# An encoder block's opening written out as one list of small operations, with form stores and K's sum column placed by hand

## Chip, cores and metric

The kernel runs on one core of a Trainium2 chip. The metric is device time in microseconds (us) of one execution; the time before is the median of 3 runs.

## What is computed

One encoder block on x of shape (1, 1024, 1024) in float32. Only the first stage bears on this change:

```python
u = rms_norm(x, norm1_g)                     # row scale, then per-column gain
proj = u @ w_in                              # 1024 x 5120
q, k, v, cb, cc, ch, ga, gb = split(proj)    # q, k, v: 512 columns each
q = rms_norm(q.reshape(B, S, 8, 64), q_norm_g)
k = rms_norm(k.reshape(B, S, 8, 64), k_norm_g)
y_a = neighbourhood_attention(q, k, v, rpb) @ w_attn_branch
...
x = x + (sigmoid(ga) * y_a + sigmoid(gb) * y_b) @ w_o
x = x + square(relu(rms_norm(x, norm2_g) @ w_mlp_in)) @ w_mlp_out
```

## The kernel before

Every float32 operand of a matmul is split into two float16 parts, high and low, and a product is three passes: high by high, high by low, low by high (`PASSES`, L473). A weight is first scaled by a power of two that is found from the weight itself: for V from the largest absolute value of the matrix (`largest`, L327), for Q and K from its sum of squares (L256 to 269). Either number is brought from 128 partitions to one by a product with an all-ones matrix (`all_sum`, L197), read back by DVE and turned into a scale.

The opening computes V, then Q, then K for the 1024 rows, in 8 blocks of 128. For each block (`norm`, L447): ACT squares and sums the row, DVE and ACT make the row scale, ACT writes the high half of the scaled row (`hi`) and DVE the low half (`lo`), into `u16`. Blocks 0 to 2 are transposed on TensorE (PE) and copied out of PSUM, the high half by ACT and the low half by DVE (`ln_trans`, L457); blocks 3 to 7 are transposed by a DMA on SP's queue (`ln_turn`, L469). The result, `UT`, is the stationary operand of everything that follows. V's weights come in two column halves of two pieces each; Q's in four pieces. V's first three blocks are computed in two half groups of 24 matmuls of 256 columns, since the second half of the weights is split later; blocks 3 to 7 in full groups of 24 matmuls of 512 columns (`v_unit`, L535); Q's and K's blocks in full groups (L643 to 652). ACT and DVE read a group out of PSUM into a high and a low part (`post`, L539).

Beside this, four "forms" are made of the scaled rows for a later stage (`sforms`, L500): ACT scales two blocks of x in place, POOL makes four sums of 512 columns, ACT and DVE split them, SP stores 1 MB to DRAM. There is one buffer for the sums and two for their split.

The order on each queue is the order in which the Python program emits instructions. It is made by generators: `bg` holds the preparation of weights (`Chunk.prep`, L250), advanced by `tick`; `fg` holds row work, forms and the read-out of Q and K (`qk_vec`, L607), advanced by `step`; `unit` (L204) emits a group of matmuls and then so many steps and ticks. `apart` (L179) holds a generator until a count of units has passed. L547 to L594 spell out the opening in such steps. Weights arrive in a ring of five buffers (`rawp`, L77; `load_upto`, L231), filled by SP in order. Waits between engines are inserted by the framework where an instruction needs another's result or a buffer.

Of the kernel before, what the change touches and what calls it, by code (L numbers as in the profile page):

```python
# [10 lines left out]
F32 = mybir.dt.float32  # L11
# [17 lines left out]
def plan():  # L29
# [19 lines left out]
    return p  # L49

# [20 lines left out]
def encoder_block(ctx: ExitStack, tc: tile.TileContext, x, weights, cols, gqk, rel, masks, out):  # L71
# [167 lines left out]
    class Chunk:  # L239
# [10 lines left out]
        def prep(self):  # L250
# [5 lines left out]
            if self.kind in "QKCG":  # L256
# [10 lines left out]
                yield from apart(units[0], 2 if self.kind in "QC" else 3)  # L267
# [179 lines left out]
    def norm(xin, sq, u, y):  # L447

        ss = tmp()
        A.activation(sq, xin, AF.Square, accum_out=sc[:, ss])  # L450
        yield
        yield from rstd(ss, D, y, 9)
        A.activation(u[:, 0], xin, AF.Copy, scale=sc[:, y])
        yield
        V.scalar_tensor_tensor(u[:, 1], xin, sc[:, y], u[:, 0], op0=OP.mult, op1=OP.subtract)

    def ln_trans(u16, b, dst):  # L457
        for s in range(2):
            pt = bank16("o")
            for k in range(8):  # L460
                T.transpose(pt[:, k * 128:(k + 1) * 128], u16[:, s, k * 128:(k + 1) * 128], ident)
            o = dst[:, s, :, b * 128:(b + 1) * 128]
            i = pt.rearrange("p (k t) -> p k t", k=8)
            if s == 0:
                A.activation(o, i, AF.Copy)
            else:
                V.tensor_copy(o, i)

    def ln_turn(u16, b, dst):  # L469
        SP.dma_start_transpose(dst[:, :, :, b * 128:(b + 1) * 128].rearrange("p s k t -> p (s k) t"),  # L470
                               u16.rearrange("p s k -> p (s k)"))

# [21 lines left out]
    ln = [norm(xt[:, b], sq, u16[:, b % 4], at(ys, b)) for b in range(8)]  # L494
    GS = dram.tile([128, 4, 4, 2, 512], F16, name="gs")

    turned, formed = [0], [0]
    SFORM = (6, 8, 10, 12)

    def sforms():  # L500

        for n, start in enumerate(SFORM):
            yield from apart(start, 0)
            assert turned[0] >= n + 5
            z = []
            for b in (n, n + 4):
                A.activation(xt[:, b], xt[:, b], AF.Copy, scale=sc[:, at(ys, b)])
                z += [xt[:, b, :512], xt[:, b, 512:]]
            f = wqk.tile([128, 4, 512], F32, name="sform", bufs=1)
            v = wqk.tile([128, 4, 2, 512], F16, name="s16", bufs=2)  # L510
            for o, a, b, op in ((2, z[0], z[2], OP.subtract), (0, z[2], z[3], OP.subtract),
                                (1, f[:, 0], z[0], OP.subtract), (3, z[1], f[:, 1], OP.add)):
                G.tensor_tensor(f[:, o], a, b, op=op)
            yield from apart(start, 2)
            A.activation(v[:, :, 0], f, AF.Copy)
            yield
            V.tensor_tensor(v[:, :, 1], f, v[:, :, 0], op=OP.subtract)
            fg.append(sform_store(n, v))

    def sform_store(n, v):  # L520
        yield from apart(units[0], 1)
        SP.dma_start(GS[:, n], v)
        formed[0] = n + 1

    def ln_step(b, n=1):
        for _ in range(n):
            advance(ln[b])
# [6 lines left out]

    def v_unit(b, j, steps, ticks):  # L535
        ps = bank("ds"[b % 2])
        n, c = (512, 0) if j is None else (256, 256 * j)

        def post():  # L539
            hi, lo = (VT[:, b, s, c:c + n] for s in range(2))  # L540
            A.activation(hi, ps[:, :n], AF.Copy, scale=2.0 ** -20)
            V.scalar_tensor_tensor(lo, ps[:, :n], 2.0 ** -20, hi, op0=OP.mult, op1=OP.subtract)
        w = vhome[0] if j is None else vhome[0][:, j]
        unit(group(ps[:, :n], [(UT[:, sa, k, b * 128:(b + 1) * 128], w[..., sw, k * 256:(k + 1) * 256])
                               for k in range(8) for sa, sw in PASSES]), post, steps, ticks)
# [12 lines left out]
    ln_step(1, 5)
    ln_step(1)
    ln_step(2, 2)  # L560
    push(cV[1])
    tick(1)
    v_unit(0, 0, 0, 0)
    ln_step(2, 4)
    ln_trans(u16[:, 1], 1, UT)
    ln_step(2, 1)
    tick(3)
    ln_step(2)
    tick(4)
    ln_step(3, 2)  # L570
    ln_trans(u16[:, 2], 2, UT)
    ln_step(3, 4)
    fg.append(qk_gain())
    fg.append(sforms())
    V.tensor_reduce(sc[:, gm2], sc[:, g1], axis=AX, op=OP.max, apply_absolute_value=True)
    mul(gm2, gm2, gm2)
    for p in range(11):
        if p == 3:
            flush()
            push(cQ)  # L580
        if 0 < p < 6:
# [1292 lines left out]
```

## Time and profile before

| | us |
|---|---|
| time, median of 3 runs | 1239.75 |
| the runs | 1237.73 to 1241.18 |
| the profiled execution's own time | 1236.77 |
| its span, first to last instruction | 1235.0 |
| PE busy | 1196.9 |
| DVE busy | 936.9 |
| ACT busy | 765.9 |
| POOL busy | 430.3 |

A view lists groups or single instructions. PE is TensorE's matmuls, PEld its weight loads, DVE VectorE, ACT ScalarE, POOL GpSimd, SP the queue that issues DMAs. A row of the view in order of time is start, duration, engine, line, operation, output<-input, shape and count; the bracket tells how long the engine stood idle before it and what ended that. L66 and L207 are lines of helpers, so operations are told apart by the names of their tiles: `xt` is x, `u` the split rows, `uT` their transpose, `w_v` and `w_ws` split weights of V and of Q or K, `vT` the split V, `sform` and `s` a form and its split. A group's row ends with total busy time, mean ns of one, and idle time before. The busy time of matmuls is modelled at their ends, so the distance between starts is the better measure.

### The profile page before, as it was taken

What the parts mean: (1) busy time and instruction counts of PE and PEld (TensorE: products, weight loads), DVE (VectorE), ACT (ScalarE), POOL (GpSimd) and SP (SyncE); (2) the same over time, 40 slices, a digit from 0 to 9 for tenths busy, and PEclk for the clock granted to TensorE, in tenths of its full rate; (3) what the DMA queues carried; (4) which work ended last, traced back from release to release, by engine and by line L of the source; (5) the groups of instructions that cost most, each with busy time, mean ns of one, the idle gap of its engine ahead of it and who ended that gap; (6) DMA issues with size and microseconds to landing.
All of it is one profiled execution on the core that took longest, in us unless ns stands there. A gap on an engine that the chain in (4) does not pass through costs nothing.

```text
span 1235.0 us, 16691 instructions
## 1 busy us (share of the span) xinstructions
PE 1196.9 (97%) x6102; PEld 576.9 (47%) x6102; DVE 936.9 (76%) x1747; ACT 765.9 (62%) x1185; POOL 430.3 (35%) x289
## 2 busy tenths in 40 slices
PE   5989999999899999999999999999999999999998
PEld 3534445555444444444458444444444444444444
DVE  6668778888558786877878664555547999999997
ACT  6777667768644454535768777777775763646430
POOL 2440003232212111101003466655648373463562
PEclk8999999999899999999999999999999999999999
DMA  6558455565761211216096653454474844435202
GB/s 258 107 200 178 103 118 112 116 153 105 131 154 34 69 52 51 69 35 255 18 174 152 205 170 137 162 187 142 140 290 162 313 155 159 168 116 222 103 35 103
DMA packets 170867, 173.34 MB, mean 140 GB/s; under 512 B 131488, under 2 KB 132000, under 8 KB 166688
## 3 DMA queue, kind: packets, MB, share of 16 engines
q1 hardware_dynamic: 170784, 172.27, 47.2%
q8 instruction: 48, 0.79, 0.3%
q14 instruction: 35, 0.29, 0.1%
HBM read 102.51 MB, written 37.75 MB: 114 GB/s over the span
## 4 chain that ended last, share of the span: by engine, by line
PE 40%; DVE 6%; ACT 2%; issue 2%; DMA 1%; DVEq 0%; ACTq 0%
PE ps_d L207 16%; PE ps_s L207 14%; PE ps_o L207 10%; DVE as L66 1%; DVE ops L66 1%; DVE w L66 1%; DVE form L66 1%; ACT as L66 1%; DVE v L66 1%; DMA u2T<-v 1%; DMA u2x<-v 1%; ACT ops L66 1%; DVE x L66 0%; DVE sc L66 0%; ACT u2x L66 0%
## 5 line engine op out<-in xcount | busy, mean ns | idle before, releaser
L207 PEld LDWEIGHTS <-ops 128*128 128x128 f16 x1356 | 132.4, 98 | 159.9 <-issue 2.7
L207 PEld LDWEIGHTS <-w 128*128 128x128 f16 x1368 | 132.8, 98 | 143.5 <-issue 3.8
L924 PE MATMUL ps_d<-uT,w_ws 128*128 128x512 f16 x576 | 136.7, 382 | 0.0
L207 PE MATMUL ps_s<-ops 128*128 128x512 f16 (+1 forms) x528 | 118.3, 374 | 0.0
L207 PE MATMUL ps_d<-ops 128*128 128x512 f16 x504 | 115.6, 379 | 0.0
L66 ACT ACTIVATE ops<-hf,sc 128x2048 f16<-128x2048 f32 x26 | 52.0, 1999 | 94.0 <-PE ps_d L207 52.7
L207 PE MATMUL ps_d<-u2T,w 128*128 128x512 f16 (+1 forms) x504 | 110.3, 371 | 0.0
L1074 POOL TENSOR_TENSOR tsum<-raw 128x512 f32<-128x512 f32 x28 | 46.6, 1677 | 148.1 <-ACT raw L66 148.1
L207 PEld LDWEIGHTS <-uT 128*128 128x128 f16 x648 | 64.9, 101 | 70.5 <-issue 5.6
L1278 POOL TENSOR_TENSOR as<-as 128x512 f32<-128x512 f32 x56 | 76.7, 1370 | 41.4 <-ACT as L66 38.1
L207 PEld LDWEIGHTS <-w_s 128*128 128x128 f16 x588 | 56.9, 98 | 68.6 <-DVE w_s L66 0.6
L924 PEld LDWEIGHTS <-w_ws 128*128 128x128 f16 x576 | 56.1, 98 | 59.7 <-issue 2.0
L207 PE MATMUL ps_s<-u2x,w 128*128 128x512 f16 (+1 forms) x348 | 78.6, 375 | 0.0
L207 PE MATMUL ps_o<-ops 128*128 128x512 f16 x324 | 74.3, 379 | 2.4 <-DVE as L66 2.4
L66 DVE SCALAR_TENSOR_TENSOR ops<-hf,sc,ops 128x2048 f16<-128x2048 f32 x26 | 71.7, 2759 | 5.7 <-ACT ops L66 5.7
L66 ACT ACTIVATE raw<-raw,sc 128x256 f32<-128x256 f32 x172 | 71.1, 494 | 6.7 <-DMA raw<-in_weights 6.7
L66 DVE TENSOR_TENSOR as<-ps_s,as 128x512 f32<-128x512 f32 (+1 forms) x38 | 23.4, 616 | 58.5 <-ACT as L66 57.9
L66 DVE TENSOR_SCALAR sc<-sc 128x1 int32<-128x1 int32 (+3 forms) x380 | 57.6, 167 | 12.9 <-ACT sq L66 4.3
L1074 POOL TENSOR_TENSOR gsum<-raw 128x512 f32<-128x512 f32 x14 | 18.5, 1340 | 136.8 <-issue 52.3
L66 ACT ACTIVATE w<-raw,sc 128x512 f16<-128x512 f32 (+1 forms) x29 | 25.4, 920 | 50.8 <-DVE sc L66 50.8
L66 ACT ACTIVATE sz<-sz,sc 128x384 f32<-128x384 f32 (+1 forms) x64 | 37.2, 581 | 26.8 <-DVE sc L66 26.6
L66 DVE SCALAR_TENSOR_TENSOR w_ws<-raw,sc,w_ws 128x512 f16<-128x512 f32 (+2 forms) x72 | 48.5, 712 | 6.7 <-ACT w_ws L66 6.7
(261 smaller groups left out, 2548.6 us busy)
## 6 DMA issues: line engine op xcount, KB each, us to landing
raw<-in_weights SPq DMA_DIRECT2D x89, 512.0 KB, 5.5
hs<-as SPq DMA_DIRECT2D x16, 1792.0 KB, 8.7
hf<-hs SPq DMA_DIRECT2D x26, 1024.0 KB, 6.7
w2x<-in_weights SPq DMA_DIRECT2D x16, 512.0 KB, 8.3
raw<-in_weights SPq DMA_DIRECT2D x16, 384.0 KB, 3.7
xt<-in_x SPq DMA_DIRECT2D x8, 512.0 KB, 9.8
gs<-s SPq DMA_DIRECT2D x4, 1024.0 KB, 6.4
x<-in_x SPq DMA_DIRECT2D x8, 512.0 KB, 10.0
```

Of the source, the lines that this page charges most:

```text
L66: return f(out, *a, **kw)
L207: T.matmul(ps, l, r, start=a, stop=b)
L924: T.matmul(ps, l, r, start=a, stop=b)
L1074: G.tensor_tensor(t[:, o], a, b, op=OP.add)
L1278: sub.tensor_tensor(z[o], z[a], z[b], op=op)
```

## The change

The generators of the opening (`norm`, `ln_trans`, `ln_turn`, `sforms`, `v_unit`, L547 to L594) go, and a string `BEGIN` names the small operations in the order in which they are emitted, V, forms and Q's first four groups together:

```text
sq.0 ts.0 sqrt.0 tr.0 y.0 tr.1 col.0 hi.0.P lo.0 Th.0 one.0 sq.1 ts.1 sq.2 scal.0 sqrt.1 y.1 ch.0.A
hi.1.P whi.0.1 whi.0.0 Tl.0 ts.2 tr.2 cl.0.V wlo.0.1.P V.0.0.hh.0 lo.1 Th.1 whi.1.0 sqrt.2 y.2 hi.2.P
whi.1.1 V.0.0.hh.1 ch.1.A sq.3 V.0.0.lh.0 V.0.0.lh.1 tr.3 Tl.1 col.1 V.1.0.hh.0 lo.2 wlo.0.0.P
V.1.0.hh.1 Th.2 cl.1.A sq.5 V.1.0.lh.0 wlo.1.0.P ch.2.V one.1 ts.3 V.1.0.lh.1 sq.4 V.2.0.hh.0 ldQ.1
scal.1 ts.5 sqrt.3 Tl.2 cl.2.V V.0.0.hl.0 ts.4 V.1.0.hl.0 y.3 whi.2.1 hi.3.P wlo.1.1. V.2.0.hh.1
V.2.0.lh.0 V.2.0.lh.1 V.2.0.hl.0 whi.2.0 V.0.1.hh.0 sqrt.4 whi.3.0 V.1.1.hh.0 y.4 lo.3 V.2.0.hl.1
V.0.0.hl.1 whi.3.1 V.2.1.hh.0 hi.4.P zs.0 wlo.2.1.P lo.4 V.1.1.hh.1 wlo.2.0. vh.0.0 vl.0.0 V.2.1.hh.1
sq.7 V.2.1.lh.0 zs.4 V.1.0.hl.1 wlo.3.0. turn.3 sqrt.5 V.1.1.lh.0 V.2.1.lh.1 qs.1 V.1.1.lh.1 vh.2.0
wlo.3.1. sq.6 ts.7 V.0.1.hh.1 V.0.1.lh.0 V.0.1.lh.1 V.0.1.hl.0 V.2.1.hl.0 y.5 ldQ.3 sqrt.7 V.1.1.hl.0
ts.6 vh.1.0 y.7 V.3..hh.0 V.3..hh.1 sqrt.6 gm2 ldQ.2 V.2.1.hl.1 V.3..lh.0 hi.5. sp.0 V.1.1.hl.1 vh.1.1
V.3..lh.1 vl.1.0 lo.5 V.0.1.hl.1 V.3..hl.0 y.6 vh.2.1 hi.6.P sh.0 zs.5 V.3..hl.1 turn.4 zs.1 vl.2.0 zs.2
V.4..hh.0 qs.3 qs.2 hi.7.P V.4..hh.1 turn.5 V.4..lh.0 V.4..lh.1 sl.0 lo.6 turn.6 lo.7 V.4..hl.0
V.4..hl.1 V.5..hh.0 V.5..hh.1 vh.0.1 vl.2.1 qs.0 V.5..lh.0 sp.1 zs.6 vh.3. vl.1.1 V.5..lh.1 V.5..hl.0
V.5..hl.1 vl.0.1 qcol qone V.6..hh.0 sh.1 qscal V.6..hh.1 V.6..lh.0 sl.1 st.0 sp.2 qhi.0.1 qhi.2.1
qlo.2.1 qhi.1.0 turn.7 qhi.1.1 qhi.0.0 qhi.3.0 zs.7 qlo.0.1 qlo.1.0 qhi.2.0 V.6..lh.1 V.6..hl.0 vh.5.
qlo.0.0 vh.4. qlo.3.0 V.6..hl.1 st.1 V.7..hh.0 qhi.3.1 qlo.2.0 V.7..hh.1 V.7..lh.0 V.7..lh.1 V.7..hl.0
qlo.1.1 ldK.1 ldK.0 V.7..hl.1 Q.0.0 sh.2 vl.4. Q.0.1 vh.6. Q.0.2 vl.3. qlo.3.1 Q.0.3 Q.1.0 Q.1.1 ldK.3
Q.1.2 zs.3 ks.0 sl.2 ks.1 sp.3 vl.5. st.2 Q.1.3 vh.7. ldK.2 qc.0 qr.0 qc.1 Q.2.0 Q.2.1 Q.2.2 qq.0 qy.0
gain sh.3 sl.3 vl.7. Q.2.3 qr.1 qc.2 Q.3.0 st.3 ks.2 ks.3 qh.0 vl.6. ql.0 Q.3.1 Q.3.2 Q.3.3 kc
```

A word is an operation with its arguments: `sq`, `ts`, `sqrt`, `y` make a row scale; `hi`, `lo` its halves; `Th`, `Tl` and `ch`, `cl` the transposes and their copies; `turn` the DMA transpose; `tr`, `col`, `one`, `scal` V's scale; `whi`, `wlo` the parts of its weights, half a piece each; `V.b.h.kind.kh` four matmuls of block b, column half h (none: full width), pass `hh`, `lh` or `hl`, first or second half of the sum; `vh`, `vl` the read-out; `qs`, `qcol`, `qone`, `qscal`, `qhi`, `qlo` the same for Q's weights; `Q.b.r` six matmuls; `qc` to `ql` the vector work on Q's groups; `zs`, `sp`, `sh`, `sl`, `st` a form's scaling, sums, high and low part and store; `ldQ`, `ldK` the next load of the ring; `ks` a square of K's weights, `kc` K's column. A trailing `P`, `A` or `V` names the engine.

```diff
-                yield from apart(units[0], 2 if self.kind in "QC" else 3)
+                yield from apart(units[0], {"Q": 2, "C": 2, "K": 1}.get(self.kind, 3))
...
     load_upto(2)
     load_x(1)
+    load_x(2)
     load_upto(4)
-    load_x(2)
     load_x(3)
+    load_x(4)
+    load_x(5)
     load_upto(5)
+    load_x(6)
+    load_x(7)
     SP.dma_start(gq.rearrange("p a d -> p (a d)"), bass.AP(tensor=gqk.tensor, offset=gqk.offset,
                                                            ap=[[0, 128], [1, 2 * HD]]))
-    for b in range(4, 8):
-        load_x(b)
...
-    def norm(xin, sq, u, y):
-    def ln_trans(u16, b, dst):
-    def ln_turn(u16, b, dst):
-    def sforms():
-    def v_unit(b, j, steps, ticks):
...
+    vw = wsp.tile([128, 2, 2, 2048], F16, name="w16_v", tag="ws")
+    cQ.parts = wsp.tile([128, 2, 4096], F16, name="w16_ws", tag="ws")
...
+    VB = 3
+    vgroups = [(b, h) for h in range(2) for b in range(VB)] + [(b, None) for b in range(VB, 8)]
...
+    def rows_square(b):
+        ss[b] = tmp()
+        A.activation(sq, xt[:, b], AF.Square, accum_out=sc[:, ss[b]])
...
+    def rows_rstd(b):
+        v, q, y = at(us[b], 0), at(us[b], 1), at(ys, b)
+        V.reciprocal(sc[:, y], sc[:, q])
+        V.scalar_tensor_tensor(sc[:, q], sc[:, y], -0.5, sc[:, y], op0=OP.mult, op1=OP.mult)
+        mul(q, v, q)
+        V.scalar_tensor_tensor(sc[:, y], sc[:, q], 1.5, sc[:, y], op0=OP.add, op1=OP.mult)
...
+    def rows_hi(b, e):
+        o, y = u16[:, b % 4, 0], sc[:, at(ys, b)]
+        if e:
+            G.tensor_scalar(o, xt[:, b], y, 1.0, op0=OP.mult, op1=OP.mult)
+        else:
+            A.activation(o, xt[:, b], AF.Copy, scale=y)
+
+    def rows_lo(b):
+        V.scalar_tensor_tensor(u16[:, b % 4, 1], xt[:, b], sc[:, at(ys, b)], u16[:, b % 4, 0],
+                               op0=OP.mult, op1=OP.subtract)
...
+    def v_col(h):
+        m = tmp()
+        mul(g1, rv[h], rv[h])
+        V.tensor_reduce(sc[:, m], sc[:, rv[h]], axis=AX, op=OP.max, apply_absolute_value=True)
+        wcol[h] = ones_col()
+        V.tensor_copy(wcol[h], sc[:, m])
+
+    def w_sum(h):
+        wbank[h] = bank("o")
+        T.matmul(wbank[h][:, 0:1], ones[:, 0:128], wcol[h], start=True, stop=True)
...
+    def v_lo(r, i, e):
+        if e:
+            t = w1p.tile([128, 512], F32, name="scaled", bufs=2)
+            for c, (w, x, s) in enumerate(v_part(r, i)):
+                G.tensor_scalar(t[:, 256 * c:256 * c + 256], x, s, 1.0, op0=OP.mult, op1=OP.mult)
+            for c, (w, x, s) in enumerate(v_part(r, i)):
+                G.tensor_tensor(w[:, 1], t[:, 256 * c:256 * c + 256], w[:, 0], op=OP.subtract)
+        else:
+            for w, x, s in v_part(r, i):
+                V.scalar_tensor_tensor(w[:, 1], x, s, w[:, 0], op0=OP.mult, op1=OP.subtract)
+        w_did(r)
...
+    def load_more():
+        load_upto(loaded[0] + 1 + held[0])
...
+    def v_mms(b, h, kind, kh):
+        g = vgroups.index((b, h))
+        if (kind, kh) == ("hh", 0):
+            vbank[g] = bank("ds"[g % 2])
+        ps = vbank[g][:, :512 if h is None else 256]
+        sa, sw = {"hh": (0, 0), "lh": (1, 0), "hl": (0, 1)}[kind]
+        for k in range(4 * kh, 4 * kh + 4):
+            w = vw[:, :, sw, k * 256:(k + 1) * 256] if h is None else vw[:, h, sw, k * 256:(k + 1) * 256]
+            T.matmul(ps, UT[:, sa, k, b * 128:(b + 1) * 128], w, start=(kind, k) == ("hh", 0),
+                     stop=(kind, k) == ("hl", 7))
...
+    def q_square(r):
+        A.activation(cQ.parts[:, 1, :1024].bitcast(BF16), cQ.raw[r], AF.Square, accum_out=sc[:, at(rq, r)])
...
+    def q_mms(b, r):
+        if r == 0:
+            vbank["q", b] = bank("ds"[(len(vgroups) + b) % 2])
+        for k in (2 * r, 2 * r + 1):
+            for n, (sa, sw) in enumerate(PASSES):
+                T.matmul(vbank["q", b], UT[:, sa, k, b * 128:(b + 1) * 128], cQ.parts[:, sw, 512 * k:512 * k + 512],
+                         start=(k, n) == (0, 0), stop=(k, n) == (7, 2))
+        units[0] += r == 3
...
+    def s_sums(n):
+        z = [xt[:, b, 512 * i:512 * i + 512] for b in (n, n + 4) for i in range(2)]
+        f = sf[n] = wqk.tile([128, 4, 512], F32, name="sform", bufs=1)
+        for o, a, b, op in ((2, z[0], z[2], OP.subtract), (0, z[2], z[3], OP.subtract),
+                            (1, f[:, 0], z[0], OP.subtract), (3, z[1], f[:, 1], OP.add)):
+            G.tensor_tensor(f[:, o], a, b, op=op)
+
+    def s_hi(n):
+        sf[n, 1] = wqk.tile([128, 4, 2, 512], F16, name="s16", bufs=2)
+        A.activation(sf[n, 1][:, :, 0], sf[n], AF.Copy)
+
+    def s_lo(n):
+        V.tensor_tensor(sf[n, 1][:, :, 1], sf[n], sf[n, 1][:, :, 0], op=OP.subtract)
...
+          "st": lambda n: SP.dma_start(GS[:, n], sf[n, 1]), "ks": lambda r: (r == 0 and push(cK), tick(1)), "kc": lambda: tick(1)}
...
+    for word in BEGIN.split():
+        name, *args = word.split(".")
+        DO[name](*[None if name in ("V", "vh", "vl") and a == "" else int(a) if a.isdigit() else a for a in args])
+
+    for b in range(4):
+        q_vec(b, 0)
+        fg.append(qv[b])
...
     for n, (kind, b) in enumerate(todo):
         ch = cQ if kind == "q" else cK
-        if b == 0:
-            push(cK if kind == "q" else cConv[0])
-        ps = bank("do"[n % 2])
-        q16[n] = []
-
-        def post(ps=ps, kind=kind, n=n, ch=ch):
-            fg.append(qk_vec(ps, ch.inv, kind, q16[n]))
-        unit(tok_mms(ps, actU, b, ch, 8, 512, 0), post, 4, 3)
-        if n == 3:
-            forced[0] = True
-            while formed[0] < 4:
-                step()
-            forced[0] = False
+        if kind == "k" and b == 0:
+            push(cConv[0])
+        if n == 4:
...
+            finish_qk(0)
+            SP.dma_start(mk, masks)
             bias = {0: bias_load(0)}
-        if n >= 3:
+        if n >= 4:
+            ps = bank("do"[n % 2])
+            q16[n] = []
+
+            def post(ps=ps, kind=kind, n=n, ch=ch):
+                fg.append(qk_vec(ps, ch.inv, kind, q16[n]))
+            unit(tok_mms(ps, actU, b, ch, 8, 512, 0), post, 4, 4 if n < 8 else 3)
             finish_qk(n - 3)
```

More of the change, by code (lines that the diff above doesn't have):

```diff
@@ new lines, in rows_hi, with rows_trans @@
+    def rows_hi(b, e):
[7 more added lines that the diff above has]
+                               op0=OP.mult, op1=OP.subtract)
+    pt = {}
+    def rows_trans(b, s):
+        pt[b, s] = bank16("o")
+        for k in range(8):
+            T.transpose(pt[b, s][:, k * 128:(k + 1) * 128], u16[:, b % 4, s, k * 128:(k + 1) * 128], ident)
```

217 lines of the change are left out of this document (113 added, 104 removed).

## The prediction

> **What bounds the kernel now.** I read the page's span first, then busy time stage by stage, then the order of time on TensorE (PE) for the first 100 us, then the first chain of DVE, ACT and POOL, and the groups by form for prices.
>
> ```profile
> span 1235.0 us, 16691 instructions
> ```
> ```profile
> 0.00:9.49 9.49, 0.00 (x0) 0.10 (x1) 4.05 (x14) 4.51 (x7) 0.44 (x5) 1.00 0.77 284
> 9.49:25.57 16.08, 10.75 (x75) 7.78 (x75) 13.84 (x35) 10.49 (x21) 5.00 (x8) 0.89 0.81 327
> 25.57:40.89 15.32, 15.04 (x122) 12.56 (x121) 10.21 (x31) 13.44 (x29) 4.41 (x8) 0.89 0.63 139
> 40.89:61.80 20.91, 20.91 (x99) 9.33 (x96) 14.02 (x29) 14.69 (x21) 10.15 (x7) 1.00 0.31 59
> ...
> 93.56:1235.00 1141.44, 1123.58 (x5692) 535.45 (x5690) 873.98 (x1612) 698.08 (x1077) 397.39 (x252) 1.00 0.47 136
> ```
> The columns are stage, length, then busy time and count of PE, PEld, DVE, ACT, POOL, then granted clock, DMA share and GB/s. From 93.56 us on PE is busy 1123.58 of 1141.44 us: that part is bound by its matmuls, and starting it earlier should move the end by the same amount. The first 93.56 us hold all that the change rewrites, and there PE has holes:
>
> ```profile
> 13.04 5.13 PE L207 MATMUL ps_d<-w_v,uT 128*128 128x256 f16 x23 [0.34 <-DVE w_v L66]
> ...
> 23.48 0.18 PE L198 MATMUL ps_o<-ones 128*128 128x1 bf16 x1 [3.53 <-DVE ones L66]
> ...
> 25.57 4.36 PE L207 MATMUL ps_s<-w_v,uT 128*128 128x256 f16 x24
> 29.77 6.05 PE L207 MATMUL ps_d<-w_v,uT 128*128 128x256 f16 x48
> 35.66 2.78 PE L207 MATMUL ps_s<-w_v,uT 128*128 128x256 f16 x24
> 38.27 2.78 PE L207 MATMUL ps_d<-w_v,uT 128*128 128x256 f16 x24
> ...
> 64.15 5.35 PE L207 MATMUL ps_s<-w_v,uT 128*128 128x512 f16 x24 [2.35 <-DMA uT<-u]
> 69.34 0.38 PE L207 MATMUL ps_d<-w_ws,uT 128*128 128x512 f16 x1
> ...
> 78.02 5.34 PE L207 MATMUL ps_o<-w_ws,uT 128*128 128x512 f16 x24
> ...
> 93.56 5.34 PE L207 MATMUL ps_d<-w_ws,uT 128*128 128x512 f16 x24
> ```
> Each row is start, duration, what ran, and in brackets the wait ahead of it. A half group of V (24 matmuls of 256 columns) costs 38.27 - 35.66 = 2.61 us undisturbed (0.109 each), a full group (24 of 512) a third of 93.56 - 78.02, 5.18. At 25.57 PE had still to do five half groups, five full V groups and Q's first four: 5 x 2.61 + 9 x 5.18 = 59.7, which would end at 85.3. Q's fourth group ended at 93.56, so 8.3 us were lost: 1.6 in the group at 25.57 (4.20 to the next start, for 2.61), 0.7 in the two after it, 2.5 ahead of 64.15 (V's last group waits for the transposed block 7), and 3.5 in Q's first group (69.34 to 78.02 for 5.18), which runs at the pace at which ACT and DVE split Q's weights. Ahead of 25.57 PE mostly waits: 10.75 busy in 16.08 us, with 3.53 idle in one piece before 23.48.
>
> **The change, part by part.** The list keeps nearly the same instructions and changes their order on every queue. What changes engine: seven of the eight high halves of the rows (hi) leave ACT for POOL; of the copies out of PSUM one low half goes to ACT and one high half to DVE (even); POOL keeps eight of the sixteen low parts of V's weights. So the gain or loss is one of order.
>
> ```profile
> 4.41 1.06 ACT L66 ACTIVATE sq<-xt 128x1024 f32<-128x1024 f32 x1 [2.18 <-DMA xt<-in_x]
> ...
> 6.92 0.15 DVE L66 RECIPROCAL sc<-sc 128x1 f32<-128x1 f32 x1
> ...
> 7.50 0.16 DVE L66 SCALAR_TENSOR_TENSOR sc<-sc 128x1 f32<-128x1 f32 x1
> ...
> 9.38 1.29 DVE L66 SCALAR_TENSOR_TENSOR u<-xt,sc,u 128x1024 f16<-128x1024 f32 x1
> ...
> 10.84 0.67 DVE L66 TENSOR_SCALAR sc<-sc 128x1 int32<-128x1 int32 x4
> 10.88 1.01 ACT L66 ACTIVATE uT<-ps_o 128x1024 f16<-128x1024 f16 x1
> ...
> 11.78 3.29 ACT L66 ACTIVATE w_v<-raw,sc 128x256 f16<-128x256 f32 x8
> ...
> 16.80 1.15 ACT L66 ACTIVATE u<-xt,sc 128x1024 f16<-128x1024 f32 x1 [1.73 <-DVE sc L66]
> ```
> ```profile
> L740 POOL TENSOR_SCALAR z<-z,sc 128x1024 f32<-128x1024 f32 x4 | 4.9, 1236 | 45.4 <-ACT sz L66 21.5 <-DVE w_ws L66 15.7 <-ACT w_ws L66 8.2
> ...
> L310 POOL TENSOR_SCALAR scaled<-raw,sc 128x256 f32<-128x256 f32 x8 | 4.1, 534 | 19.3 <-DVE sc L66 10.5 <-issue 8.8
> ```
> *Start.* Block 0's square at 4.41 and its scale at 7.66 stay. hi of block 0 on POOL has no row of its own; the nearest is 1024 elements times a column, 1.24 (the bounds are 1.15, ACT's row, and 4 x 0.53 = 2.1 by the 256-element pieces; I take 1.24, the same shape). It ends near 9.0; the low half still follows V's column on DVE (9.38 now) and ends near 10.75. V's scale (it ends at 10.84 + 0.67 = 11.51 now) then ends near 11.8. New is that block 1's scale follows at once: four small DVE operations, 0.75 by 6.92 to 7.66, so 12.6, and its hi on POOL ends near 13.9, where ACT now finished it at 16.80 + 1.15 = 17.95. That lead of 4 us is the start's whole gain: DVE no longer writes four low parts of weights between V's scale and block 1's. From there ACT sets the step: copy of block 0 (1.0), then the four weight halves of the first piece (0.41 each by the row at 11.78), so the first V quarter starts near 14.1; block 1's high copy ends near 16.8; its low transposes near 19.2 (two quarters of four slow matmuls and eight transposes of about 0.1 later); their copy, on ACT, near 20.3; the second all-ones product (one.1) leaves PE near 21.8 (before: 23.66). I take 20.5 to 24.5 as its ends: all waits zero, or the present time plus a copy.
>
> *PE from there.* By one.1 the list has done 28 of the 144 half-width matmuls and five of the six sets of transposes. What remains is 116 x 0.109 + 0.6 + 9 x 5.18 = 59.9, so Q's fourth group ends at 81.7 if nothing is late. Slow clock: 23 matmuls in 5.13 at 13.04 are 0.22 each, twice the later price, and the 3.5 us of idle before 23.48 brought that price back until 29.77. The list has no idle piece that long after 14 us; I add 0.6, ends 0 and 2.5 (all 23 of the next matmuls slow).
>
> *Waits on the way.* The list's order on DVE, with these prices:
>
> ```profile
> L66 DVE TENSOR_TENSOR s<-sform,s 128x2048 f16<-128x2048 f32 x4 | 9.1, 2287 | 7.5 <-ACT s L66 7.5
> ...
> L66 DVE TENSOR_REDUCE sc<-raw 128x4 f32<-128x1024 f32 x4 | 4.9, 1214 | 0.0
> ...
> L66 DVE SCALAR_TENSOR_TENSOR w_v<-raw,sc,w_v 128x256 f16<-128x256 f32 x8 | 4.1, 575 | 0.0
> ...
> L66 DVE COPY uT<-ps_o 128x1024 f16<-128x1024 f16 x3 | 2.1, 689 | 0.7 <-PE ps_o L461 0.7
> ```
> ```profile
> DMA to landing us min/median/max: 4.2/4.3/5.5
> ```
> Block 1's low half ends near 15.9. Then come two row scales (0.75), a maximum (1.21), V's second column (0.5) and scale (0.9), two copies (0.69), a pair of weight low parts (1.1), two more row scales and the low halves of blocks 2 and 3 (1.29 each): some 11, so block 3 at 27 and block 4 at 29 behind it. Block 5's high half waits on ACT for four Q and row squares and is out at 35.5, its low half at 37. Blocks 6 and 7 stand behind the first form's low half (2.29), which ends near 42 (ACT's 1.91 ahead of it starts near 38, behind two read-outs of V that PE frees at 37): 44 and 45. A transpose lands up to 5.5 later: 32, 35, 42, 49 and, with a 1 MB form store ahead of block 7's, 52. PE wants them at 34, 40, 46, 51 and 56. So the 2.5 us ahead of 64.15 go. SP's first Q load waits for V's piece until about 21 and holds nothing, since the transpose behind it is not due until 27.
>
> *Q's split.* ACT must reach Q's last square before PE reaches Q's product, and its high parts before Q's first group.
>
> ```profile
> L66 ACT ACTIVATE sq<-xt 128x1024 f32<-128x1024 f32 x8 | 8.4, 1045 | 2.3 <-DMA xt<-in_x 2.2
> L66 ACT ACTIVATION_READ_ACCUMULATOR sq<-xt 128x1 f32 x8 | 1.5, 188 | 0.0
> L66 ACT ACTIVATE vT<-ps_d 128x256 f16<-128x256 f32 x4 | 1.5, 366 | 0.0
> L66 ACT ACTIVATE s<-sform 128x2048 f16<-128x2048 f32 x4 | 7.6, 1910 | 8.0 <-POOL sform L513 6.6 <-DMA gs<-s 1.4
> ```
> ```profile
> 44.75 2.17 ACT L66 ACTIVATE xt<-xt,sc 128x1024 f32<-128x1024 f32 x2
> ...
> 68.07 2.56 ACT L66 ACTIVATE w_ws<-raw,sc 128x512 f16<-128x512 f32 x4 [0.42 <-DVE sc L66]
> ...
> 68.83 2.71 DVE L66 SCALAR_TENSOR_TENSOR w_ws<-raw,sc,w_ws 128x512 f16<-128x512 f32 x2 [0.79 <-ACT w_ws L66]
> ```
> The last row is two low parts of Q beside POOL; I take 0.9, below the 1.36 of that row because the second form's sums are over by then. Up to the last square ACT has twelve squares of 1.23, sixteen weight parts of 0.41, three copies of 1.0, five scaled blocks of 1.09, one hi 1.15, six half read-outs 0.37, one form 1.91, eight roots 0.2: 36.6. From 4.41 and with some 6 us of waits it is there at 47; PE arrives at 51. To the last high part come two scaled blocks, a form, three full read-outs (at most twice 0.37 each) and eight parts of 0.64, 11.4 more: 59 or so with the wait for the product. DVE, from 45: three read-outs (1.3), Q's column, then the scale when PE has given the product (52.4), the second form's low half (2.29), seven low parts of Q at 0.9, two read-outs (0.7), the last low part: 63. Q's first group starts at 61.5 and needs that part at 65.4. So the 3.5 us of Q's first group go too.
>
> *Form stores and K.* The stores keep one per form and lie on SP between transposes with slack as above. K's squares and column stand in the list, and the product comes out after Q's fifth group, as it does now; with four ticks instead of three K's split is reached earlier. I cost both at nothing; the cover is Q's groups 5 to 8, 4 x 5.18. Without it K's split (four parts of about 0.64 and their low halves) would cost about 3.5, like Q's now.
>
> *Sum.* 81.7 + 0.6 + waits that I did not find, 1.2 (ends 0 and 6, the whole of what the engines wait for now between 61 and 78) = 83.5 against 93.56: **10 us less**. On the profile's own span, 1235.0 becomes 1225; its execution took 1236.77, under the median of 1239.75, which becomes 1229.8.
>
> **The rivals.**
>
> ```profile
> L66 DVE SCALAR_TENSOR_TENSOR u<-xt,sc,u x8: 1284/1285/2319, 9.4 to 58.2; 128x1024 f16<-128x1024 f32 x8
> L513 POOL TENSOR_TENSOR sform<-xt x4: 1271/1276/2252, 47.0 to 58.7; 128x512 f32<-128x512 f32 x4
> ```
> *POOL and DVE slow each other.* Both rows are minimum, median, maximum: a low half of a row takes 1.28 alone and 2.32 where POOL's form sums run, and the sums stretch from 1.27 to 2.25. POOL now works from 8 us on, beside most of DVE's two-input operations. If the seven low halves after the first each cost 1.04 more, DVE is 7.3 us later. Its last low part of Q, near 63 by my sum, comes at 70 where PE wants it at 65.4: 4.9 lost, time 1234.7. Against it: one in eight was stretched so. The Trainium skill, "GPSIMD Engine Reference", Specifications, says that GpSimd shares its SBUF interface with VectorE and contends with DVE instructions with two SBUF inputs, which speaks against this change; the two maxima above agree with it, and by that rule the time would be this rival's.
>
> *The slow clock lasts.* The list issues V in quarters with a wait after most of them. If PE stayed at 0.22 per half-width matmul until block 3, the 116 remaining ones cost 116 x 0.114 = 13.2 more: 1229.8 + 12.6 = 1242.4, no change that can be told. For it: clock 0.89 from 9.49 to 40.89 even now. Against: it recovered within 4.2 us at 25.57, in a group without waits.
>
> *ACT sets the end (the other side).* The list ties ACT to PE (read-outs between quarters) and to POOL (forms ahead of Q's parts). The waits ACT may have between 4.41 and 65.4 are 65.4 - 4.41 - 48.0 = 13.0; each us beyond stalls PE at Q's product or first group. Now ACT is idle 61.80 - (4.51 + 10.49 + 13.44 + 14.69) = 18.7 in the first 61.8 us, at least 14.3 of it after 4.41, so idle time like today's is already past that limit by 1.3; it takes 13 + 10 + 3.7 = 27 us of waits to be slower than noise. With 29 the time is 1245. Against it: much of today's idle time is the start, which shrinks by 4.
>
> *It does not do what it says* (the planned order is moved back by other waits): 1239.8, counted with no change.
>
> **How the numbers follow.** Forecast (a gain of 7.5 to 13) 0.58; stretched DVE and POOL (a gain of 4 to 7.5) 0.20; slow clock or no effect 0.10; ACT 0.10; better than 13, 0.02. About 0.3%, 3.7 us, is what a measurement of this kernel can tell from no change. Faster 0.80, same 0.10, slower 0.10. The ends of the terms give 20.5 instead of 21.8 and no waits or slow clock, 3.1 less (1226.7), and 24.5, 2.5 and 6 together 9.4 more (1239.2). With the spread of the runs I set 1226 to 1238, which leaves out about 0.17.
>
> **What would show it.** Right: PE without an idle piece over 2 us after 22; one.1 near 22; V's last group with no wait on a DMA; Q's first group in about 5.2; Q's fourth ending at 82 to 85, and the rest still about 1141 long. Wrong: PE waiting on Q's column or parts, row operations on DVE well over 1.3, a granted clock under 0.9 past 25, or a rest longer than 1143 us.

## The result and the profile after

The changed kernel takes 1233.11 us (median of 4 runs, 1232.89 to 1233.94) against 1239.47 for the kernel before on the same chip (1237.73 to 1241.18): ratio 0.995, 95% interval 0.9933 to 0.9967. That is 6.4 us faster where 10 was forecast. The profiled execution took 1232.89.

First the head line of the page, then the busy time by stage (columns as in the prediction), with the boundaries of the table shown of before.

```profile
span 1231.1 us, 16698 instructions
```
```profile
9.49:25.57 16.08, 13.43 (x116) 11.31 (x115) 14.55 (x44) 14.67 (x33) 12.06 (x15) 1.00 0.77 299
...
40.89:61.80 20.91, 20.91 (x100) 9.34 (x98) 17.37 (x24) 17.77 (x25) 15.70 (x9) 1.00 0.73 182
```
Between 9.49 and 25.57 us PE is busy 13.43 instead of 10.75 us, ACT 14.67 instead of 10.49 and POOL 12.06 instead of 5.00: all three get more done in the same time. From 40.89 to 61.80 PE is as full as before, so the lead was made ahead of it and in the two holes behind it. The order of time on PE shows where:

```profile
13.98 1.20 PE L665 MATMUL ps_d<-w_v,uT 128*128 128x256 f16 x4 [1.77 <-ACT w_v L89]
...
20.89 0.17 PE L618 MATMUL ps_o<-ones 128*128 128x1 bf16 x1
...
34.75 0.68 PE L665 MATMUL ps_s<-w_v,uT 128*128 128x256 f16 x3
36.56 0.27 PE L665 MATMUL ps_s<-w_v,uT 128*128 128x256 f16 x1 [1.13 <-DVE w_v L89]
...
56.59 5.35 PE L665 MATMUL ps_d<-w_v,uT 128*128 128x512 f16 x24
61.78 0.38 PE L708 MATMUL ps_s<-w_ws,uT 128*128 128x512 f16 x1
62.89 2.10 PE L708 MATMUL ps_s<-w_ws,uT 128*128 128x512 f16 x9 [0.73 <-DVE w_ws L89]
...
68.91 5.34 PE L708 MATMUL ps_d<-w_ws,uT 128*128 128x512 f16 x24
...
79.27 5.34 PE L708 MATMUL ps_d<-w_ws,uT 128*128 128x512 f16 x24
...
89.63 0.17 PE L221 MATMUL ps_s<-ones 128*128 128x1 bf16 x1
...
105.52 0.38 PE L230 MATMUL ps_d<-w_ws,uT 128*128 128x512 f16 x1 [0.16 <-ACT w_ws L89]
...
112.03 2.73 PE L230 MATMUL ps_d<-w_ws,uT 128*128 128x512 f16 x11 [1.50 <-DVE w_ws L89]
114.59 5.34 PE L230 MATMUL ps_o<-w_ws,uT 128*128 128x512 f16 x24
```
The all-ones product at 20.89 is the second one of V (before: 23.48). The group at 79.27 is Q's fourth; it ends at 84.45, where before ended at 93.56: **9.1 us of lead**. V's last group, at 56.59, has no wait for a DMA. The two rows at 34.75 and 36.56 show four matmuls that take 1.92 us instead of 0.44, behind a low part of V's weights on DVE. Q's first group still lasts 68.91 - 61.78 = 7.13 us instead of 5.18.

Then half of the lead goes. K's first group follows Q's eighth at 84.45 + 4 x 5.18 = 105.2, and K's second starts only at 114.59: 9.4 us for 5.18 of work, **4.2 us lost**. In the kernel before K's first group ran through (114.30 to 119.48). So the lead is 119.48 - 114.59 = 4.9 us there, and from there to the end it is 1235.0 - 119.48 = 1115.5 us before and 1231.1 - 114.59 = 1116.5 after.

What K's first group waited for is in the order of time on ACT and DVE. On ACT (first fence) the first row is the high parts of Q's blocks 1 and 2, the second that of block 3, the last two K's weights, two pairs of high parts each; on DVE (second) the reading of K's product, the low part of Q's block 3, and the next steps of K's scale:

```profile
91.21 2.00 ACT L89 ACTIVATE q<-qs 128x1024 f16<-128x1024 f32 x2 [1.08 <-DVE qs L89]
...
98.90 1.06 ACT L89 ACTIVATE q<-qs 128x1024 f16<-128x1024 f32 x1 [5.68 <-DMA qD<-q]
...
104.76 2.54 ACT L89 ACTIVATE w_ws<-raw,sc 128x512 f16<-128x512 f32 x4
...
109.39 2.54 ACT L89 ACTIVATE w_ws<-raw,sc 128x512 f16<-128x512 f32 x4
```
```profile
95.18 0.15 DVE L89 TENSOR_SCALAR sc<-ps_s 128x1 f32<-128x1 f32 x1
...
99.99 1.23 DVE L89 TENSOR_TENSOR q<-qs,q 128x1024 f16<-128x1024 f32 x1 [4.66 <-ACT q L89]
...
101.83 0.34 DVE L89 TENSOR_SCALAR sc<-sc 128x1 int32<-128x1 int32 x3
```
And in the kernel before the same of Q on ACT, blocks 0 to 3, with K's first high parts behind them:

```profile
91.82 1.06 ACT L66 ACTIVATE q<-qs 128x1024 f16<-128x1024 f32 x1 [0.38 <-DVE qs L66]
...
95.67 1.06 ACT L66 ACTIVATE q<-qs 128x1024 f16<-128x1024 f32 x1 [0.38 <-DVE qs L66]
...
99.80 1.06 ACT L66 ACTIVATE q<-qs 128x1024 f16<-128x1024 f32 x1 [0.67 <-DVE sc L66]
...
103.72 1.06 ACT L66 ACTIVATE q<-qs 128x1024 f16<-128x1024 f32 x1 [0.44 <-DVE qs L66]
...
110.58 2.54 ACT L66 ACTIVATE w_ws<-raw,sc 128x512 f16<-128x512 f32 x4
```
K's first high parts stood 114.30 - 110.58 = 3.7 us ahead of K's first group; now, at 104.76, they start 0.4 us ahead of the 105.2 at which it is due. ACT idles 5.68 us at 98.90 for `DMA qD<-q`: there are two buffers for the split of Q's blocks, each is free only when SP's transpose of the block in it has landed, and block 3's high part takes block 1's buffer. Before, block 3's came 103.72 - 95.67 = 8.0 us after block 1's, and found it free; now ACT would write it 2 us after block 1's (91.21 + 2.00 = 93.2), since in the new order the high parts of blocks 1 and 2 come out together (the list itself ends with block 0's; the generators behind it emit the next ones). DVE idles 4.66 us behind ACT. And DVE reads K's product at 95.18, 5.4 us after PE made it, since the generator lets one more unit pass; what K's scale and split still need of DVE and ACT then stands behind that wait, from 101.83 on.

### The profile page after: what moved, and what is told of

Same layout as the page of the kernel before. It is cut to its first block, busy times and chain, and to the rows that moved or that the text cites. A ratio compares the mean times of both kernels' runs of the same rounds, so it can differ in the third digit from the quotient of the medians.

```text
span 1231.1 us, 16698 instructions
## 1 busy us (share of the span) xinstructions
PE 1194.8 (97%) x6102; PEld 575.3 (47%) x6102; DVE 941.0 (76%) x1747; ACT 757.5 (62%) x1178; POOL 444.6 (36%) x296
## 4 chain that ended last, share of the span: by engine, by line
PE 60%; DVE 9%; ACT 3%; issue 2%; DMA 0%; DVEq 0%; ACTq 0%
PE ps_d L230 23%; PE ps_s L230 21%; PE ps_o L230 16%; DVE sg L89 2%; DVE sc L89 1%; DVE w_s L89 1%; DVE ops L89 1%; DVE as L89 1%; DVE w L89 1%; ACT ops L89 1%; ACT w_s L89 0%; ACT as L89 0%; DVE m L89 0%; ACT sg L89 0%; DMA PT<-P 0%
## 5 line engine op out<-in xcount | busy, mean ns | idle before, releaser
L230 PE MATMUL ps_o<-u2T,w 128*128 128x512 f16 (+1 forms) x204 | 45.7, 375 | 2.4 <-DVE as L89 2.4
```

The lines of the kernel that those rows point to most:

```text
L230: T.matmul(ps, l, r, start=a, stop=b)
```

## The experiments

"K's second group" is its start on PE; 114.59 in the changed kernel's profile, 119.48 before. The medians of the kernel before, measured beside the experiments, were 1239.3 (13 runs), 1239.84 (27) and 1238.92 (13).

**The changed kernel and the one before, again.** No edit.

> The changed kernel once more, beside the three that follow on the same chip. Expected near 1233.1 us, with Q's fourth group ending near 84.5 us and K's first group lasting about 9 us (5.18 undisturbed).

> The kernel before, with a second profile. Its profiled execution took 1236.77 us where its median is 1239.3, the changed kernel's 1232.89 and 1231.94 at a median near 1233. If the difference of 2.5 us is a short stretch of slow clock at the one place of 2.4 us where PE waits for DVE near 946 us (as in the profiles of the four-buffer and the late-form run, granted 0.66 there, 12 matmuls in 4.4 us instead of 2.6), a profile of about 1239 to 1240 shows it there; a profile of about 1237 shows none. If not, a slow execution shows its extra time elsewhere.

The changed kernel: 1232.63 (1231.94 to 1232.99, 4 runs), ratio 0.9945 (0.9931 to 0.996); Q's fourth group ends at 83.86, K's second starts at 113.52. The kernel before: 1240.61 (1237.51 to 1244.67, 10 runs). Its profiled execution took 1244.35, 7.6 us more than the first one shown, and differs in the granted clock (the third number from the end of a row of the table by stage) and in the time of matmuls far behind the change:

```profile
710.00:715.00 5.00, 4.96 (x16) 1.93 (x16) 0.59 (x1) 4.35 (x4) 0.27 (x1) 0.66 0.42 169
...
952.85 4.44 PE L207 MATMUL ps_o<-ops 128*128 128x512 f16 x12 [2.38 <-DVE as L66]
```
```profile
710.00:715.00 5.00, 4.21 (x22) 1.81 (x20) 2.24 (x10) 2.58 (x5) 3.70 (x3) 1.00 0.00 0
...
948.51 2.75 PE L207 MATMUL ps_o<-ops 128*128 128x512 f16 x12 [2.38 <-DVE as L66]
```
The upper fence is this execution, the lower the first. The same twelve matmuls take 4.44 or 2.75 us after the same wait of 2.38 (granted clock 0.84 from 950 to 955 us and 0.82 from 955 to 960 in the upper one, 1.00 in the lower). K's second group starts at 120.29 here, so 0.8 of the 7.6 us lie ahead of it and 6.8 behind it. One program thus takes 1236.8 or 1244.4 us, and the difference of two single profiles is no measure of a change of this size; the medians are.

**What K's first group waits for.** Three edits: two more buffers for the split of Q's blocks 2 and 3 (taken from the tile of the forms, idle there); K's product read as soon as it is emitted; K's product emitted one unit earlier, where it stands before Q's fifth group.

```diff
-        t = wqk.tile([128, 8, 2, r, HD], F16, name=kind + "16", tag="q16")
+        if spare:
+            t = wqk.tile([128, 4, 2, 512], F16, name="s16", bufs=2)
...
-            qv[b] = qk_vec(vbank["q", b], cQ.inv, "q", q16[b])
+            qv[b] = qk_vec(vbank["q", b], cQ.inv, "q", q16[b], b > 1)
```


> Only edit: the split parts of Q's blocks 2 and 3 go into the forms' two buffers, which are free by then, so that the first four blocks have four buffers and block 3's high part no longer waits for block 1's transpose to land. Theory W (that wait holds ACT 5.7 us and DVE 4.7 us, with K's scale and split queued behind it): no wait of ACT on the transposes between 90 and 100 us, K's first group 5.2 to 5.7 us long in place of 9.2, time 3.5 to 4 us below the changed kernel, 1229.1 to 1229.6. Theory P (K's split is late because its all-ones product is emitted behind Q's fifth group and read behind the sixth): K's first group stays at 8 to 9 us, time within 0.7 us of 1233.1.

```diff
-                yield from all_sum(c, b, bank(self.bank) if self.bank else anybank(), 1e-36)
+                yield from all_sum(c, b, bank(self.bank) if self.bank else anybank(), 1e-36,
+                                        0 if self.kind == "K" else 1)
```


> Only edit: DVE reads K's all-ones product one unit earlier than the changed kernel does, so K's scale and split are emitted some three ticks earlier; the buffers stay as they are. Theory P: K's first group 5.2 to 5.7 us long, time 1229 to 1230. Theory W: the read comes at about 90 us in place of 95.2, but the split's high parts stay behind block 3's high part on ACT, which waits until 98.9, so the first starts at 100 to 103 us; with K's first group due at 105.2 that leaves a stall of 0 to 2 us, time 1229 to 1231. The two theories part here only by ACT's wait, which W expects unchanged at 5 to 6 us.

```diff
-                yield from apart(units[0], {"Q": 2, "C": 2, "K": 1}.get(self.kind, 3))
+                yield from apart(units[0], {"Q": 2, "C": 2, "K": 0}.get(self.kind, 3))
```


> Only edit: K's all-ones product is emitted with K's column, ahead of Q's fifth group, instead of one unit on. DVE writes that column near 87.3 us and Q's fourth group ends near 84.5, so PE should stand 2.5 to 3 us ahead of Q's fifth group; the reading and the split move up by one unit, so the stall of 4.0 us in K's first group should shrink to 0 to 1.5. Time within 1.5 us of the changed kernel, 1231.5 to 1234. If the place of the product doesn't bear on the split, the stall stays at 4 us and the time is 1235.5 to 1236.

K's first group and the start of the second on PE, with four buffers (first fence) and with the product read at once (second):

```profile
105.71 5.34 PE L230 MATMUL ps_d<-w_ws,uT 128*128 128x512 f16 x24
110.89 5.34 PE L230 MATMUL ps_o<-w_ws,uT 128*128 128x512 f16 x24
```
```profile
104.72 4.26 PE L230 MATMUL ps_d<-w_ws,uT 128*128 128x512 f16 x19
...
110.48 5.34 PE L230 MATMUL ps_o<-w_ws,uT 128*128 128x512 f16 x24
```
Either edit alone brings the group back to 5.18 and 5.76 us. With four buffers ACT's wait on the transposes is gone; with the early reading it is still there (DVE stands 4.10 behind it), but K's product is read at 89.39, more of K's scale is done ahead of the wait, and K's first high parts start at 101.66 instead of 104.76, so it hardly hurts. So the loss needs both, the wait on Q's buffers and K's scale and split queued behind it. The times: 1231.76 (1228.85 to 1232.69), ratio 0.9931 (0.991 to 0.9953), with four buffers; 1229.87 (1228.09 to 1231.67), ratio 0.9924 (0.9903 to 0.9944), read at once; 4 runs each. The second gives 2.8 us of the 4.2 back, the first only 0.9 by the medians, which the spread of its four runs doesn't tell from nothing, though its PE is 3.7 us ahead at 110.89. In its profile the time from there to the end is 1230.9 - 110.89 = 1120.0 us instead of 1116.5. Half of that shows at a hand-off far behind, the same matmuls in the changed kernel (first fence) and with four buffers (second):

```profile
944.64 2.75 PE L230 MATMUL ps_o<-ops 128*128 128x512 f16 x12 [2.38 <-DVE as L89]
```
```profile
941.57 4.44 PE L230 MATMUL ps_o<-ops 128*128 128x512 f16 x12 [2.40 <-DVE as L89]
```
Twelve matmuls are busy 4.44 instead of 2.75 us, 1.7 lost; the granted clock from 940 to 945 us is 0.66. The four executions with the early reading stand in two pairs, 1228.1 and 1228.3, 1231.5 and 1231.7, and the profiled one is of the slower pair.

Emitting the product earlier gives 1233.86 (1232.72 to 1239.45, 10 runs), ratio 0.9962 (0.9949 to 0.9976), no gain on the changed kernel: PE waits 2.71 us for DVE's column ahead of the product (86.92), and K's first group, with 5.73 us from 107.68, starts as much later. The product cannot move ahead of its column.

**What Q's first group waits for.** The third form's scaling and sums (`zs.6`, `sp.2`) stand behind Q's last high part instead of ahead of the first; its split and store, and the read-outs and the fourth form's split near them, come later too.

```diff
-V.5..lh.0 sp.1 zs.6 vh.3.
...
-sl.1 st.0 sp.2 qhi.0.1
...
+V.5..lh.0 sp.1 vh.3.
...
+sl.1 st.0 qhi.0.1
...
+V.7..hh.0 qhi.3.1 zs.6 sp.2 qlo.2.0
```


> Only edit: the scaling of block 6 moves behind Q's last high part, so that POOL's sums of the third form start near 62 us in place of 57 and run behind most of Q's low parts; the third form's split and the read-outs next to it follow. Theory C (POOL's sums and DVE's two-input operations stretch each other, and that is what is lost in Q's first group): Q's low parts take 0.7 to 0.75 us in place of 1.25, Q's first group 5.2 to 5.7 us in place of 7.1, time 1.3 to 1.9 us below the changed kernel. Rival (Q's low parts are late because the second form's low part stands ahead of them on DVE): the parts start no earlier, Q's first group stays at 6.5 us or more, time within 0.7 us.

Q's low parts on DVE and the form's sums on POOL in the changed kernel, then the same low parts here, and what follows on PE:

```profile
57.06 8.78 DVE L89 SCALAR_TENSOR_TENSOR w_ws<-raw,sc,w_ws 128x512 f16<-128x512 f32 x7
57.22 3.40 POOL L729 TENSOR_TENSOR sform<-xt 128x512 f32<-128x512 f32 x2 [4.35 <-DVE s L89]
```
```profile
56.62 4.72 DVE L87 SCALAR_TENSOR_TENSOR w_ws<-raw,sc,w_ws 128x512 f16<-128x512 f32 x7
```
```profile
61.40 5.34 PE L706 MATMUL ps_s<-w_ws,uT 128*128 128x512 f16 x24
...
88.66 0.16 PE L219 MATMUL ps_s<-ones 128*128 128x1 bf16 x1 [1.20 <-DVE ones L87]
...
106.06 0.38 PE L228 MATMUL ps_d<-w_ws,uT 128*128 128x512 f16 x1 [1.68 <-ACT w_ws L87]
...
115.14 5.34 PE L228 MATMUL ps_o<-w_ws,uT 128*128 128x512 f16 x24
```
Seven low parts take 8.78 us (1.25 each) beside POOL's sums and 4.72 (0.67 each) without them. Q's first group is back at 5.18 us, Q's fourth ends at 82.12, 2.3 earlier. But DVE's column of K is now 1.20 late (88.66), K's high parts 1.68 (106.06), and K's second group starts at 115.14: what Q gained K lost, and the time is 1235.26 (1233.46 to 1237.92, 10 runs), ratio 0.9967 (0.9953 to 0.998), 2.6 more than the changed kernel beside it. Only 0.55 of that is there when K's second group starts; from there to the end this profile takes 1235.2 - 115.14 = 1120.1 us instead of 1116.5, which no run explains. A hole closed ahead of a queue that is late anyway moves the hole.

**All three edits together**, the late third form, four buffers and the early reading:

> The three edits of the runs before together: two more buffers for Q's parts, K's product read one unit earlier, the third form behind Q's low parts. If the three losses are separate (W: buffers and place of the reading; C: POOL against DVE), Q's fourth group ends near 82.1 us, the product waits about 1.2 us for K's column, K's first group is 5.2 us long, K's second starts near 109.4 (119.48 in the kernel before, 114.4 in the changed one) and the time is 5 us below the changed kernel, 1227 to 1229. If the third form's delay only moves the loss (rival), K's first group is 7 us or longer and the time is 1231 or more.

K's first group takes 5.18 us and the second starts at 110.91, though V's first quarter was 0.9 later in this execution. Time 1230.55 (1228.93 to 1231.86, 5 runs), ratio 0.993 (0.9917 to 0.9942): beyond the changed kernel, but above the 1227 to 1229 expected and no better than the early reading alone, which is the smallest edit that keeps the lead.

**Where the lead comes from.** Three more: the list with the seven high halves of the rows back on ACT; the kernel before with those seven on POOL and nothing else changed; the changed kernel with the loads of x in their old order.

```diff
-hi.0.P hi.1.P hi.2.P hi.3.P hi.4.P hi.6.P hi.7.P
+hi.0. hi.1. hi.2. hi.3. hi.4. hi.6. hi.7.
```


> Only edit: the seven high halves of the rows go back from POOL to ACT, at the same places of the list. If POOL's high halves stretch DVE's two-input operations enough to matter, DVE's low parts of V's second half (1.2 us each now, 0.58 on average in the kernel before) fall to 0.6, PE's wait of 1.1 us for them goes, and Q's fourth group ends at 82.5 to 84.0 in place of 84.5. Rival, ACT has no room: its queue gets 7 x 1.1 us longer, PE waits for copies and parts, and Q's fourth group ends at 86 to 90, time 1235 to 1239.

```diff
-        A.activation(u[:, 0], xin, AF.Copy, scale=sc[:, y])
+        if y.start == ys.start + 5:
+            A.activation(u[:, 0], xin, AF.Copy, scale=sc[:, y])
+        else:
+            G.tensor_scalar(u[:, 0], xin, sc[:, y], 1.0, op0=OP.mult, op1=OP.mult)
```


> The kernel before with one thing changed: the high halves of the first seven blocks of the split of x are made by POOL (block 5's stays with ACT), everything else in the old order. Theory M (most of the lead at the end of Q's first four groups is that these seven instructions leave ACT): Q's fourth group ends between 85 and 89 us instead of 93.6, and the time is 1233 to 1235.5. Rival O (they help only in the new list's order): Q's fourth group ends within 1.5 us of 93.6 and the time is within 1.5 us of the kernel before.

```diff
+    load_upto(4)
     load_x(2)
-    load_upto(4)
...
+    load_upto(5)
     load_x(4)
     load_x(5)
-    load_upto(5)
```


> The changed kernel with the loads of x issued in the order of the kernel before. Theory L (the order of the loads is worth something at the start): the first quarter of V starts 0.5 to 1.5 us later than 9.3 and Q's fourth group ends at 84.5 to 86, time +0 to +1.5 us on the changed kernel. Rival N (the loads have slack): Q's fourth group ends within 0.5 us of 84.45 and the time is within 0.5 us of 1233.

(V's first quarter starts at 13.98 in the changed kernel; 9.3 is the start of block 0's transposes.)

*The list without POOL's halves* takes 1239.62 (1237.76 to 1244.94, 10 runs), ratio 1.0007 (0.9994 to 1.0019): all of the gain is gone. V's first quarter starts at 15.82, the second all-ones product at 26.02, PE waits 2.23 us for Q's column ahead of its product (58.83), and Q's fourth group ends at 91.62, 7.2 late. PE's wait for the low parts of V's second half is gone, as expected (they take 2.68 us for four instead of 4.79), but ACT has no room, beyond the rival's figures. Q's fourth group is still 1.9 us ahead of the kernel before, and K then loses 4.1: its second group starts at 121.64, and ACT waits for the same buffers:

```profile
105.96 1.06 ACT L87 ACTIVATE q<-qs 128x1024 f16<-128x1024 f32 x1 [5.57 <-DMA qD<-q]
```

*The halves without the list* take 1244.96 (1244.6 to 1245.45, 4 runs), ratio 1.0046 (1.0029 to 1.0063). Both theories missed: Q's fourth group ends at 101.36, and it is slower than before. POOL's order and PE's waits:

```profile
14.83 2.84 POOL L298 TENSOR_TENSOR w_v<-scaled,w_v 128x256 f16<-128x256 f32 x4 [0.43 <-ACT w_v L66]
17.79 1.12 POOL L456 TENSOR_SCALAR u<-xt,sc 128x1024 f16<-128x1024 f32 x1
...
52.90 1.26 POOL L516 TENSOR_TENSOR sform<-xt,sform 128x512 f32<-128x512 f32 x1
54.14 1.12 POOL L456 TENSOR_SCALAR u<-xt,sc 128x1024 f16<-128x1024 f32 x1
...
66.82 1.12 POOL L456 TENSOR_SCALAR u<-xt,sc 128x1024 f16<-128x1024 f32 x1
```
```profile
60.91 6.74 PE L207 MATMUL ps_d<-w_v,uT 128*128 128x512 f16 x24 [3.47 <-DMA uT<-u]
73.59 7.21 PE L207 MATMUL ps_s<-w_v,uT 128*128 128x512 f16 x24 [5.95 <-DMA uT<-u]
```
Block 1's half (17.79) stands behind the weights' low parts that POOL makes there, and ends at 18.91, no earlier than ACT's had (17.95). Blocks 6 and 7 (54.14, 66.82) stand behind the sums of the first and second form, so their transposes land late and PE waits 3.47 and 5.95 us, with 6.74 and 7.21 us for groups that otherwise take 5.34 (granted clock 0.66 from 60 to 65 us, 0.56 and 0.76 from 70 to 80). Neither the place alone nor the list alone shows a gain in time; the two together are worth 6.4. A list ordered for the halves on ACT was not tried.

*The old order of the loads* costs 3.7: 1236.85 (1235.32 to 1239.82, 10 runs), ratio 0.9981 (0.9971 to 0.9992). Rival N is out, and theory L's size was too small.

```profile
13.69 1.06 ACT L89 ACTIVATE sq<-xt 128x1024 f32<-128x1024 f32 x1 [2.68 <-DMA xt<-in_x]
...
14.75 0.19 ACT L89 ACTIVATE sc<-sc 128x1 f32<-128x1 f32 x1
```
```profile
17.09 1.20 PE L665 MATMUL ps_d<-w_v,uT 128*128 128x256 f16 x4 [4.31 <-ACT w_v L89]
```
The list puts block 2's square (13.69) ahead of block 1's root (14.75) on ACT, and in the old order block 2 lands 2.68 us after ACT wants it. Block 1's scale, the copy of block 0 and V's weights queue behind: V's first quarter starts at 17.09 instead of 13.98, and Q's fourth group ends at 87.56, the same 3.1 later. K's first group then loses 4.0, as in the changed kernel (its second starts at 117.42).

## Why the prediction was right or wrong

**Start.** Right within a us. Block 0's high half on POOL took 1.12 us (1.24 taken), block 1's stood at 12.70 to 13.82 (13.9), V's first quarter at 13.98 (14.1), the second all-ones product ended at 21.06 (21.8). But the loads were not weighed: that start hangs on the new order of x's loads, by 3.1 us, and the prediction has no term for them.

**PE from there.** The 59.9 us held: 84.45 - 21.06 = 63.4 us, of which 1.48 were lost around 36.56 and 1.95 in Q's first group; 60.0 are left. The slow clock, 0.6, did not come: from 21 us on half-width matmuls take 0.109.

**Waits on the way.** V's last group has no wait, as forecast. The wait at 36.56 was not seen ahead:

```profile
31.72 4.79 DVE L89 SCALAR_TENSOR_TENSOR w_v<-raw,sc,w_v 128x256 f16<-128x256 f32 x4
31.96 2.87 POOL L729 TENSOR_TENSOR sform<-xt 128x512 f32<-128x512 f32 x2
```
Four low parts of V's weights take 1.2 us each, priced 0.575, beside POOL's first form sums.

**Q's split** is a mis-sized term: the product came out at 51.35 (51), but the last low part ended at 66.96 + 0.73 = 67.7 (63). About half of that is that the seven before it took 1.25 each instead of 0.9: the prediction reckoned with the second form's sums alone, which are over by then, and the list emits the third's, `sp.2`, just ahead of Q's parts. The other half is that they began at 57.06 (54.7): DVE stood 1.95 us for ACT's high part of the second form, which had stood 3.02 for POOL's sums, and ahead of those one of the moved high halves took POOL 3.15 us instead of 1.12. The late start alone costs PE nothing, as the late third form shows (parts from 56.62 at 0.67, Q's first group 5.18). With 1.2 us set aside for waits and 3.4 measured, less 0.6 and 0.7 gained elsewhere, Q's fourth group ended 0.95 later than the 83.5 of the sum; that it came so close is in part that these errors cancel.

**Form stores and K** is the step that failed: "I cost both at nothing; the cover is Q's groups 5 to 8". It cost 4.2, close to the 3.5 that the prediction gave for the case without cover. The cover was counted in PE's time, four groups, and not in that of the queues: the read-out of Q's blocks, bunched in the new order, ran into the landing time of SP's transposes, so ACT and DVE met a wait for buffers that the kernel before did not have there, and K's scale and split stood behind it. Two edits that remove one link each restored the group (5.18 and 5.76 us). That Q's groups come earlier is not the cause: with the halves on ACT Q's fourth group ends only 1.9 us ahead of the kernel before, and K loses the same 4.1.

**The sum.** A lead of 9.1 instead of 10, less 4.2 at K, is 4.9; spans 1235.0 and 1231.1 differ by 3.9, the medians by 6.4. The second profiles of the two kernels put K's second group at 120.29 and 113.52, a lead of 6.8, so the lead is known to about 1 us either way. From there to the end the kernel before took 1115.5 and 1122.3 us, the changed one 1116.5 and 1116.7. The 2.5 between the first profiles and the medians are argued, not shown: the first profile of before is among its fastest executions (1236.77, where executions from 1235.95 to 1244.67 were seen), while the eight of the changed kernel lie within 2 us. What decides whether an execution of either kernel meets the slow spots was not settled. That the time lies in the range of 1226 to 1238 is owed to the width of the range: a gain of 6.4 falls not in the forecast's own band of 7.5 to 13 but in the 4 to 7.5 that was given to POOL and DVE with 0.20, and it got there by another way, K's 4.2.

**The signs.** Of those named ahead, no idle piece of PE over 2 us between 22 us and Q's fourth group, the second all-ones product near 22, V's last group without a wait and Q's fourth ending at 82 to 85 came true. Q's first group in 5.2 did not (7.13, with PE waiting for Q's parts), and the rest took 1231.1 - 84.45 = 1146.6 us, past the 1143 that was named as a sign of being wrong; 4.2 of that is K.

**The rivals.** *POOL and DVE slow each other* came true in part. It priced seven low halves of rows at 1.04 more; two of those nearly were (4.35 us for the pair, with no wait on PE behind it), the median of the eight low halves is 1.39 instead of 1.29; what PE felt were the low parts of weights, for 1.48 + 1.95 us. The rule of the Trainium skill that it rests on ("GPSIMD Engine Reference", Specifications: POOL shares its SBUF interface with VectorE and contends with two-input DVE instructions) agrees with the trace, 1.25 against 0.67 us. It forbids nothing here: the stretched pairs cost 3.4 us, and ACT's room bought with POOL is worth 7. *ACT sets the end* did not happen, because of POOL: with the halves on ACT it does, for 7.2 us. *The slow clock lasts* did not happen.

## What to carry to other kernels

When the order of a stretch is written anew, ask of each later step not how much PE time covers it but which buffers and DMAs its queues wait for in the new order: results that come out together need as many free buffers, and steps that everyone needs (here those of a scale) should not stand behind that wait. Moving work to an idle engine and writing out the order are one change here, not two: either alone lost 6 to 12 us against both together. A list that fixes the order of operations also fixes which loads must come first.

## What was not expected of the hardware

PE waits 2.4 us for DVE at two places far behind the change (near 700 and 945 us), in both kernels, and after such a wait the granted clock of a window of 5 us sometimes falls to 0.66 and sometimes not: in the two profiles of the kernel before, the twelve matmuls after the wait of 2.38 us near 950 take 2.75 and 4.44 us; at 945 us it is 1.00 in the changed kernel's profile and 0.66 with four buffers, after 2.38 and 2.40 us of waiting. Such a fall costs about 1.7 us there, and the executions of one kernel differ by which they meet. Near 330 us PE waits for a DMA (`PT<-P`), and that wait differs too: 2.49 and 4.11 us in the two profiles of the kernel before, 4.43 and 2.32 in those of the changed one. The Trainium skill, "TensorE: Matmul & The Clock Gate", Part 1, has the gate judge activity in windows of some 3.4 us that run on by themselves. It has the clock fall after at least one idle window; here a wait of 2.4 us, which is shorter, was enough in some executions, so the measurement decides. Windows that run on by themselves would fit a wait that is sometimes enough, by where it falls in a window, but no run here moved a wait against the window to show it.
